# The last store of a transfer-bound kernel, cut into three parts by partitions

## Chip, core and metric

The kernel runs on one core of a Trainium2 chip. The metric is the device time of one execution in microseconds (us). The clock granted was 1.0. The experiments ran in three groups, each on a chip of its own together with the kernel before, so a time is compared with the kernel before "of its rounds".

## The reference

The inputs `y` and `dy` are fp32 tensors of shape 8 x 1024 x 8192, that is 8192 rows of 8192 numbers. The output has the same shape.

```python
softmax_x = np.exp(y)
sum_dy = np.sum(dy, axis=-1, keepdims=True)
return (dy - softmax_x * sum_dy).astype(np.float32)
```

Two tensors of 268 MB are read and one is written, and each number is used in a handful of operations: 805 MB pass through the transfer engines.

## The kernel before

The 8192 rows are 32 groups of 256 rows. A group fills a tile of 128 partitions, two rows in each, so a partition holds 64 KB that are contiguous in memory as well. Two tiles `x0` and `x1` take `dy` and become the output in place; one tile takes `y`. All transfers are issued by one queue. Only the end of the loop matters here.

```python
out_v = out.flatten_outer_dims().rearrange("(g p r) d -> g p (r d)", p=P, r=R)   # P = 128, R = 2
# ... loads, sums and pieces of exp and multiply-add cut ...
for g in range(0, G, 2):
    # ... x_ts[0] and x_ts[1] are loaded and computed ...
    for j in range(2):
        nc.sync.dma_start(out=out_v[g + j], in_=x_ts[j][:])
```

## Time and profile before

| | before |
|---|---|
| median of 4 runs | 1867.63 us (1866.89 to 1867.79) |
| transfers | 99.9% of 16 engines' span, 432 GB/s |
| VectorE, ScalarE busy | 46%, 37% |
| vector engine done with the last tile | 1837.9 us in the trace |
| first and last completion signal of the last store | 1861.20 and 1865.06 us |

The lines behind this are in the prediction below. Two further windows of the trace of the kernel before are the yardstick for later: start and end of the window in us, its length, three busy times, the clock, the share of the 16 transfer engines, GB/s.

```profile
1842.00:1846.00 4.00, 0.00 (x0) 0.00 (x0) 0.00 (x0) 1.00 0.91 393
1846.00:1850.00 4.00, 0.00 (x0) 0.00 (x0) 0.00 (x0) 1.00 1.02 442
```

No compute runs any more, and the last store flows at the full rate, 418 GB/s over the two windows. A packet is counted where it starts, so a short window may read somewhat high or low.

### The profile page before, as it was taken

How to read it: one execution, taken by the hardware profiler on the slowest of the kernel's cores; microseconds unless marked ns; L12 is line 12 of the kernel's file. 1: busy time of each engine (PE TensorE's matmuls, PEld its weight loads, DVE VectorE, ACT ScalarE, POOL GpSimd, SP SyncE). 2: the span in 40 equal slices, each digit the busy share in tenths (PEclk: the TensorE clock that was granted, in tenths of full speed). 3: DMA queues.
4: the chain of work that ended last, by engine and by line, in shares of the span. 5: the costliest groups of instructions: out<-in, count | busy, mean ns of one | idle time of the engine just before them, and what ended most of it. 6: DMA issues, size and time to landing. Idle time of an engine off the chain costs nothing.

```text
span 1865.9 us, 923 instructions
## 1 busy us (share of the span) xinstructions
DVE 859.8 (46%) x256; ACT 698.7 (37%) x321; POOL 0.2 (0%) x4
## 2 busy tenths in 40 slices
DVE  2907429074290732807328073280632806338063
ACT  2606326063260532605336052360523605236052
POOL 0000000000000000000000000000000000000000
DMA  9999999999999999999999999999999999999999
GB/s 427 424 430 427 430 447 427 427 431 445 427 427 441 426 437 434 438 431 427 437 438 429 433 428 440 434 431 437 425 438 436 433 436 425 439 433 436 434 428 391
DMA packets 16135, 805.37 MB, mean 432 GB/s; under 512 B 1792, under 2 KB 1792, under 8 KB 1792
## 3 DMA queue, kind: packets, MB, share of 16 engines
q1 hardware_dynamic: 16128, 805.31, 99.9%
q14 instruction: 7, 0.06, 0.0%
HBM read 536.87 MB, written 268.44 MB: 432 GB/s over the span
## 4 chain that ended last, share of the span: by engine, by line
DMA 64%; DVE 13%; ACT 10%; another core or an unknown queue 9%; issue 1%; SPq 0%; DVEq 0%; ACTq 0%
DMA x<-in_dy_dram 31%; DMA out_dram<-x 30%; DVE x L81 13%; ACT copied L61 6%; ACT y_t L80 4%; DMA y_t<-in_y_dram 3%; SPq L75 0%; DVEq L128 0%; ACTq L128 0%; SPq L52 0%; ACTq L80 0%; ACTq L61 0%
## 5 line engine op out<-in xcount | busy, mean ns | idle before, releaser
L81 DVE SCALAR_TENSOR_TENSOR x<-y_t,s_t,x 128x3072 f32<-128x3072 f32 (+1 forms) x192 | 579.4, 3059 | 255.7 <-ACT y_t L80 255.7
L57 DVE TENSOR_REDUCE s_t<-x 128x1 f32<-128x8192 f32 x32 | 277.8, 8682 | 722.3 <-DMA x<-in_dy_dram 722.3
L80 ACT ACTIVATE y_t<-y_t 128x3072 f32<-128x3072 f32 (+1 forms) x192 | 460.1, 2466 | 269.4 <-DMA y_t<-in_y_dram 253.2
L61 ACT ACTIVATE copied<-x 128x4096 f32<-128x4096 f32 x64 | 229.6, 3587 | 864.9 <-DMA x<-in_dy_dram 863.9
L61 ACT ACTIVATION_READ_ACCUMULATOR copied<-x 128x1 f32 x64 | 11.9, 186 | 0.0
L64 DVE TENSOR_SCALAR s_t<-half_t 128x1 f32<-128x1 f32 x32 | 6.5, 204 | 0.0
L61 ACT ACT_TABLE_LOAD x1 | 1.3, 1283 | 0.7 <-PEq L117 0.7
L117 POOL MEMSET const-bfloat16-1.0<- 128x1 bf16 x1 | 0.1, 101 | 0.0
L117 POOL MEMSET const-uint8-127<- 128x1 uint8 x1 | 0.1, 101 | 0.0
L117 POOL MEMSET const-float32-0.0<- 128x1 f32 x1 | 0.1, 98 | 0.2 <-issue 0.2
L117 POOL MEMSET const-float32-1.0<- 128x1 f32 x1 | 0.1, 98 | 0.0
## 6 DMA issues: line engine op xcount, KB each, us to landing
y_t<-in_y_dram SPq DMA_DIRECT2D x32, 4096.0 KB, 18.1
x<-in_dy_dram SPq DMA_DIRECT2D x32, 48.3
out_dram<-x SPq DMA_DIRECT2D x32, 32.5
y_t<-in_y_dram SPq DMA_DIRECT2D x16, 57.6
```

Source lines behind the costliest of these rows:

```text
L57: nc.vector.tensor_reduce(out=s_t[:, 0:1], in_=x[:, :D], axis=mybir.AxisListType.X, op=ALU.add, negate=True)
L61: nc.scalar.activation(copied[:], x[:, D + h * H : D + (h + 1) * H], COPY, accum_out=half_t[:, h : h + 1])
L64: nc.vector.tensor_scalar(out=s_t[:, 1:2], in0=half_t[:, 0:1], scalar1=half_t[:, 1:2], scalar2=-1.0, op0=ALU.add, op1=ALU.mult,)
L80: nc.scalar.activation(y_t[:, cs], y_t[:, cs], EXP)
L81: nc.vector.scalar_tensor_tensor(out=x[:, cs], in0=y_t[:, cs], scalar=s_t[:, r : r + 1], in1=x[:, cs], op0=ALU.mult, op1=ALU.add,)
L117: nc = _bacc.Bacc("TRN2", target_bir_lowering=False, num_devices=1)
```

## The change

As far as the edit shows, the intent is balance at the end. The 16 transfer engines stop 3.9 us apart; if the late engine is the one that is left out, it gets less of the last store. 15 partitions on 15 engines leave one out, 112 partitions give seven to each of the 16, and the last partition is meant to be divided evenly.

```diff
-        for j in range(2):
-            nc.sync.dma_start(out=out_v[g + j], in_=x_ts[j][:])
+        nc.sync.dma_start(out=out_v[g], in_=x_ts[0][:])
+        if g + 2 < G:
+            nc.sync.dma_start(out=out_v[g + 1], in_=x_ts[1][:])
+        else:
+            nc.sync.dma_start(out=out_v[g + 1][0:15], in_=x_ts[1][0:15, :])
+            nc.sync.dma_start(out=out_v[g + 1][15 : P - 1], in_=x_ts[1][15 : P - 1, :])
+            nc.sync.dma_start(
+                out=out_v[g + 1][P - 1 : P].rearrange("p (e w) -> p e w", e=16),
+                in_=x_ts[1][P - 1 : P, :].rearrange("p (e w) -> p e w", e=16),
+            )
```

## The prediction

The terms of its sum came to about 10 us more than before: 7.25 for the first part, about 3.5 for the second, less up to 0.75 for balance; the third part was put at 2.42 at most and left out. They were estimates. The unit is the packet of 2.418 us in the trace of before: 7.25 us are the three further packets if four take turns (4 x 2.418 = 9.67 us instead of 2.42), and about 3.5 is the middle of 2 to 5, for one or two such turns. Balance was put at -0.75 us if the late engine is the one left out (it has one packet less, but the next engine is only 0.92 us ahead of it, and gets a sixteenth of the last partition) and +0.2 if not. That packets take turns was not shown then. "Port" is, here and in all that follows, a name for whatever packets of several engines share when they slow each other.

> **What bounds the kernel now.** I read the page first: engines, slices, queues.
>
> ```profile
> span 1865.9 us, 923 instructions
> ...
> DVE 859.8 (46%) x256; ACT 698.7 (37%) x321; POOL 0.2 (0%) x4
> ...
> DMA  9999999999999999999999999999999999999999
> GB/s 427 424 430 427 430 447 427 427 431 445 427 427 441 426 437 434 438 431 427 437 438 429 433 428 440 434 431 437 425 438 436 433 436 425 439 433 436 434 428 391
> ...
> q1 hardware_dynamic: 16128, 805.31, 99.9%
> ```
>
> The reader is to see that no compute engine is busy for half of the span, and that the 16 transfer engines together are busy for 99.9% of it. 805 MB over 1865.9 us is 432 GB/s from the first slice to the last but one. So compute time, waits and issue order are hidden; only two things set the time: how many bytes one transfer engine has to move and how fast it moves them, and how unevenly the 16 engines stop. The trace's transfer records give the unit: a 64 KB row (one partition of a group: two rows of 8192 fp32) is one packet, and 2.418 us is the common duration of one, load or store, which is 65,536 B / 2.418 us = 27.1 GB/s per engine and 16 x 27.1 = 434 GB/s for all. A group of 128 partitions is 8 such packets per engine, 19.3 us.
>
> Then the end, which is all that the change touches: first the waits of the store queue from 1700 us on, then short windows from 1838 us on (the last two columns are the transfer engines' share and GB/s, counted by the packets that start in the window).
>
> ```profile
> SPq L128 <- DMA out_dram<-x: 26.6, 2, 19.2
> ```
>
> ```profile
> 1850.00:1855.00 5.00, 0.00 (x0) 0.00 (x0) 0.00 (x0) 1.00 1.03 446
> 1855.00:1860.00 5.00, 0.00 (x0) 0.00 (x0) 0.00 (x0) 1.00 0.97 419
> 1860.00:1861.00 1.00, 0.00 (x0) 0.00 (x0) 0.00 (x0) 1.00 0.76 328
> 1861.00:1862.00 1.00, 0.00 (x0) 0.00 (x0) 0.00 (x0) 1.00 0.15 66
> 1862.00:1863.00 1.00, 0.00 (x0) 0.00 (x0) 0.00 (x0) 1.00 0.15 66
> 1863.00:1864.00 1.00, 0.00 (x0) 0.00 (x0) 0.00 (x0) 1.00 0.00 0
> ```
>
> The vector engine is done with the last tile at 1837.9 us; from there the program only waits for its two last stores, 19.2 us for the second. 66 GB/s over 1 us is one 64 KB packet: from 1860 to 1861 us five packets start, then one, then a last one alone after 1862 us. The 16 completion signals of that store in the trace say the same finer: the first engine signals at 1861.20 us, the last but one at 1864.14, the last at 1865.06. The engines end 3.86 us apart. The last one is 0.92 us behind the next, and only that lone stretch is there to be won by unloading one engine. The spread was 0.65 us after the first load and grew by small irregular delays; each engine moved the same number of bytes.
>
> [...]
>
> **The change, part by part.** Bytes are the same. Issue: two stores become four; the store issues of before took 344 and 432 ns, so the two added ones cost some 0.8 us of the issuing queue, starting at 1837.9 us, while the engines are busy with the store before until 1841.9 us or later: hidden.
>
> [...]
>
> [...] Sum: 7.25 + about 3.5, less up to 0.75 of the gain, so about 10 us as the full estimate, and 6 to 7 if the second part brings no meetings.
>
> **The rivals.** (1) *The ports bind*: +6 to +12 us. [...] Against it: nothing in this trace shows a port at its limit apart from its engine, and whoever made the change expected 15 engines to run side by side. I give it 55%. (2) *The ports do not bind for reads*: only balance counts, -0.8 us if the late engine is the one unloaded, +0.2 us if not. For it: the engine's own rate explains all that is seen in before. 37%. (3) *The ports bind and the shares of the second part are interleaved* (engine e takes every sixteenth partition): [...] +25 us or more. Against it: 16 neighbours at once would be a poor way to split[...]. 8%. A new wait of the queue or of compute as the bound is out: nothing is computed after 1837.9 us, and the engines have 4 us of work queued when the parts are issued.
>
> **Range and chances.** The time before is 1867.58 us, with runs from 1866.89 to 1867.79, so noise is under 1 us. Rival 2 gives 1866.8 to 1867.8, rival 1 1873.5 to 1879.5, rival 3 about 1893 or more. The two main outcomes have a hole between them. The middle of my distribution lies at the low edge of rival 1, and I place the point there: 1873 us. The range, 1866 to 1881, holds rivals 2 and 1 whole. Two per cent is 37 us: no gain of that size exists, since the whole spread of the engines is 3.9 us, and only a bad form of rival 3 could lose it. So within 2% is all but certain.
>
> **What would show it.** In the changed kernel's trace look at the packets that start after 1838 us. If ports bind, up to 15 packets of 64 KB last toward 9.7 us instead of 2.42, the GB/s of the windows from 1842 to 1852 us falls to a third, and one engine's completions come many us before the others'. If they do not bind, every 64 KB packet stays at 2.42 us[...], and the spread of the last completions shrinks from 3.86 us to about 3. [...] The page's counts should rise by the packets of the split: 128 rows become 127 rows and 16 pieces, and the completions from 16 to 15 + 16 + 16. The prediction is wrong [...] if a packet's duration shows a sharing cost between the two cases (half-shared ports), or if the time falls by more than 1 us.

## The result

The changed kernel takes 1882.70 us (median of 4 runs, 1882.23 to 1884.27) against 1867.63 us: 15.1 us more. The ratio is 1.0083, with a 95% interval of 1.0065 to 1.0100. Ratios here are the mean time of one kernel's runs over that of the other's runs of the same rounds, so not quite the ratio of the medians. By the 2% rule it is the same; by the noise of this kernel, under 1 us in the runs before, it is clearly slower.

The page of the changed kernel first: the rate in 40 equal slices of the time, then the queue.

```profile
GB/s 423 423 425 433 434 446 424 440 425 437 436 430 439 424 444 425 444 425 439 430 437 429 433 433 432 430 436 437 429 439 427 441 430 434 432 429 439 432 437 231
...
q1 hardware_dynamic: 16144, 805.31, 99.6%
```

Only the last slice of 47 us differs: 231 GB/s where it was 391. The bytes are the same, so the whole loss lies in that slice, which reaches to the new end. The queue's packet count gives away one more thing. It rose by 16, from 16128. A store of 128 rows on 16 engines is 128 + 16 = 144 packets, data and completions; the new parts give 15 + 15, 112 + 16, and for the last partition either 16 + 16 or 1 + 1. Only the last choice makes 160. So the view as 16 pieces did not survive: the row, contiguous on both sides, went as one packet of 64 KB on one engine.

Next, what the store queue waits for from 1700 us on, and windows over the end, of the changed kernel. The first line is the waiting for the last stores: 42.8 us in total, where the kernel before had 26.6. That is 16.2 of the 16.6 us by which the two profiled runs differ.

```profile
SPq L137 <- DMA out_dram<-x: 42.8, 2, 39.5
```

```profile
1842.00:1846.00 4.00, 0.00 (x0) 0.00 (x0) 0.00 (x0) 1.00 1.15 197
1846.00:1850.00 4.00, 0.00 (x0) 0.00 (x0) 0.00 (x0) 1.00 0.43 147
1850.00:1855.00 5.00, 0.00 (x0) 0.00 (x0) 0.00 (x0) 1.00 0.82 275
1855.00:1860.00 5.00, 0.00 (x0) 0.00 (x0) 0.00 (x0) 1.00 1.10 315
1860.00:1865.00 5.00, 0.00 (x0) 0.00 (x0) 0.00 (x0) 1.00 0.75 249
1865.00:1870.00 5.00, 0.00 (x0) 0.00 (x0) 0.00 (x0) 1.00 0.83 275
1870.00:1875.00 5.00, 0.00 (x0) 0.00 (x0) 0.00 (x0) 1.00 0.53 170
1875.00:1880.00 5.00, 0.00 (x0) 0.00 (x0) 0.00 (x0) 1.00 0.13 52
```

From 1842 to 1850 us, when the first part is in flight, the rate is (197 + 147) / 2 = 172 GB/s instead of 418. Later it is 249 to 315, until 1870 us, and does not come back. The share column is higher than the rate suggests (a mean of 0.79 over these two windows, with 172 GB/s): the engines are occupied, but their packets are slow. In the transfer records 99 of 100 packets of 64 KB before the last store take at most 2.43 us; the 15 of the first part take 3.3 to 14.1 us, and many of the second part lie near 5.1 us, twice the normal.

The trace also lets one engine be recognised: after the store before, exactly one engine goes on with a packet of 2.42 us, where 15 have a slow one. It must be the one without a share in the first part; the trace has no engine numbers. It finished the store before at 1842.42 us, 1.26 us ahead of the last engine. In this execution the late engine was another one.

### The profile page after: what moved, and what is told of

Read it like the earlier page. It is cut to its first block, busy times and chain, and to the rows that moved or that the text cites. A ratio compares the mean times of both kernels' runs of the same rounds, so it can differ in the third digit from the quotient of the medians.

```text
span 1882.5 us, 925 instructions
## 1 busy us (share of the span) xinstructions
DVE 859.9 (46%) x256; ACT 698.7 (37%) x321; POOL 0.2 (0%) x4
## 4 chain that ended last, share of the span: by engine, by line
DMA 64%; DVE 13%; ACT 10%; another core or an unknown queue 9%; issue 1%; SPq 0%; DVEq 0%; ACTq 0%
DMA x<-in_dy_dram 31%; DMA out_dram<-x 30%; DVE x L81 13%; ACT copied L61 6%; ACT y_t L80 4%; DMA y_t<-in_y_dram 3%; SPq L75 0%; DVEq L137 0%; ACTq L137 0%; SPq L52 0%; ACTq L80 0%; ACTq L61 0%
```

## The experiments

**Theory A** says that the reading of the partitions is shared: some partitions lie on one port, a port delivers one 64 KB packet per 2.42 us (the time of a packet in the trace of before) whoever asks, and the parts send several engines to one port. Which partitions those are is for the probes to show. **Theory B** says that the places of the rows in memory collide. **Theory C** says that more transfers in the queue cost. **Theory D** says that the uneven shares make the time, above all the ninth packet on the engine that got the single row.

### A probe: stores alone, one at a time

The kernel's loop is replaced by one load and then single stores of 64 KB rows, each after the one before has landed. Its output is wrong, which doesn't matter for the time.

```diff
-    for g in range(0, G, 2):
-        ... (the whole loop)
+    x = x_ts[0]
+    o = out_v[G - 1]
+    load_dy(0, x)
+    for rep in range(2):
+        gate()      # a small write to the tile, which waits for the store before it
+        nc.sync.dma_start(out=o[0:128], in_=x[0:128, :])
+        gate()
+        nc.sync.dma_start(out=o[0:15], in_=x[0:15, :])
+        gate()
+        nc.sync.dma_start(out=o[36:93:4], in_=x[36:93:4, :])
+        gate()
+        nc.sync.dma_start(out=o[0:15], in_=x[36:93:4, :])
+        gate()
+        nc.sync.dma_start(out=o[36:93:4], in_=x[0:15, :])
+        ... (further sets in the same way)
```

> A probe, wrong result on purpose: one load, then stores of 64 KB rows one at a time, each waiting for the one before, twice over. Each is told by the time its packets take, between issue and completion; some 2 us of fixed time lie on top. Theory A (the SBUF ports are shared: a port gives 27.1 GB/s, one packet alone 2.42 us): 128 partitions 19.3 us of packets; 15 neighbouring partitions 9.7; 15 partitions 36,40,..,92[...], 2.4, whether their rows go to neighbouring places in HBM or to spread ones; 15 neighbouring partitions to spread rows in HBM still 9.7; 112 partitions from 15 or from 0 about 22 instead of 17; 16 neighbours 9.7; 4 neighbours (one port) 9.7, 4 partitions on four ports 2.4. Theory B (the rows' places in HBM collide, not the ports): what decides is the destination: neighbouring rows slow whatever the source, spread rows fast even from neighbouring partitions. Theory C (the queue or the number of transfers costs): all sets of 15 or 16 the same 2.4. The partition as 16 pieces in one transfer: one packet of 64 KB on one engine, 2.4 us, as the trace of the changed kernel suggests; as two transfers of 16 separate 2 KB pieces: spread over 16 engines. The last two are loads into the 15 neighbouring and the 15 spread partitions: theory A 9.7 and 2.4.

The windows from one issue to the next, in this order: 128 partitions; 15 neighbours; 15 spread (36, 40, up to 92); spread partitions to neighbouring rows in memory; neighbouring partitions to spread rows in memory; the 112 of the change; the single partition as in the change. The columns are as before, with two busy times instead of three.

```profile
22.84:43.81 20.97, 0.07 (x1) 0.00 (x0) 1.00 0.93 400
43.81:55.52 11.71, 0.07 (x1) 0.00 (x0) 1.00 0.75 84
55.52:60.24 4.72, 0.07 (x1) 0.00 (x0) 1.00 0.49 208
60.24:64.90 4.66, 0.07 (x1) 0.00 (x0) 1.00 0.50 211
64.90:76.60 11.70, 0.07 (x1) 0.00 (x0) 1.00 0.75 84
76.60:100.48 23.88, 0.07 (x1) 0.00 (x0) 1.00 0.85 307
...
168.14:171.66 3.52, 0.00 (x0) 0.00 (x0) 1.00 0.04 19
```

The four middle comparisons are the case in small. The source decides (11.7 against 4.7 us) and the destination changes nothing (11.71 and 11.70; 4.72 and 4.66). Theory B is out, and so is theory C for this transfer, since all four move 15 rows on 15 engines (15 data packets and 15 completions in the windows of both sets). The packets alone, without the fixed time around them, take 19.54, 10.31, 2.59, 2.59, 10.31 and 22.48 us in the order of the first six windows. Beside seven eighths of 19.54 = 17.10 us, the 112 partitions are 5.4 us slow. In windows that are not printed 16 neighbours took 11.72 us, four neighbours (0 to 3) 11.54, and four in steps of four (0, 4, 8, 12) 4.36. So 0 to 3 share a port, those four in steps of four do not, and 15 or 16 neighbours take as long as four at one port: I call them a four-port part, an estimate from these times. The trace shows the single partition as one data packet of 2.45 us and one completion; sent as two transfers of 16 separated 2 KB pieces it became 32 data packets. The same holds for loads: into the 15 neighbours 9.7 us of packets, into the 15 spread partitions 3.35, a little more than the 2.4 expected.

### The same end with one thing undone

**The single row truly on 16 engines.**

```diff
-            nc.sync.dma_start(
-                out=out_v[g + 1][P - 1 : P].rearrange("p (e w) -> p e w", e=16),
-                in_=x_ts[1][P - 1 : P, :].rearrange("p (e w) -> p e w", e=16),
-            )
+            for h in range(2):
+                nc.sync.dma_start(
+                    out=out_v[g + 1][P - 1 : P].rearrange("p (e h w) -> p e h w", e=16, h=2)[:, :, h],
+                    in_=x_ts[1][P - 1 : P, :].rearrange("p (e h w) -> p e h w", e=16, h=2)[:, :, h],
+                )
```

> As the change, but the last partition goes as two transfers of 16 separated 2 KB pieces each, so that it truly runs on 16 engines. Theory A (shared ports): the third part is a bystander, since its single packet ended 3 us before the last one of the second part; 1880 to 1884 us, within 1 us or so of the changed kernel's 1882.7. Theory D (the ninth packet on one engine makes the time): 2.4 us or more of the 15 come back, 1880 us or less.

It took 1884.30 us (ratio to before 1.0092, 1.0077 to 1.0107), no better than the change and 0.3 us over the range expected for a bystander (1880 to 1884). Spreading the lone packet wins nothing back.

**Equal shares on all 16 engines.**

```diff
-            ... (the three parts)
+            nc.sync.dma_start(out=out_v[g + 1][0:16], in_=x_ts[1][0:16, :])
+            nc.sync.dma_start(out=out_v[g + 1][16:128], in_=x_ts[1][16:128, :])
```

> The last store in two parts, partitions 0 to 15 and 16 to 127, each on all 16 engines with equal shares: no engine is unloaded, no single row. Theory A: still about 12 us or more over the kernel before, 1878 to 1885 us[...]. Theory D (unequal shares, k = 15 or the single row): like the kernel before, 1867 to 1868 us.

It took 1883.53 us (1.0090, 1.0073 to 1.0107). Here no engine is unloaded and none has a ninth packet, if the 16 and the 112 are shared equally, as the 112 are in the changed kernel's trace (seven packets in each chain); and the loss is all there. (k = 15 in the expectation means the 15 engines of the first part.) Theory D is out: the cost does not come from the balance. Whether the uneven shares gain a little is not shown, since the intervals of the two ratios overlap and 0.75 us is too small to tell.

**Two parts by columns.**

```diff
-            ... (the three parts)
+            for h in range(2):
+                nc.sync.dma_start(
+                    out=out_v[g + 1][:, h * D : (h + 1) * D], in_=x_ts[1][:, h * D : (h + 1) * D]
+                )
```

> The last store in two parts by columns: all 128 partitions in each, half of the row each. [...] Theory A: 1867 to 1868 us, as the kernel before. Theory C (more transfers in the queue at the end cost): slower by several us.

It took 1866.81 us, beside 1866.96 for the kernel before in the same rounds (ratio 0.9999, 0.9984 to 1.0014). One more transfer at the end cost nothing here, where each transfer holds all 128 partitions.

**Two parts by partitions.** The same number of transfers, each over half of the partitions.

```diff
-            ... (the three parts)
+            nc.sync.dma_start(out=out_v[g + 1][0:64], in_=x_ts[1][0:64, :])
+            nc.sync.dma_start(out=out_v[g + 1][64:128], in_=x_ts[1][64:128, :])
```

> The last store as partitions 0 to 63 and 64 to 127: two equal transfers on all 16 engines, as many transfers as by columns (1866.8 us)[...]. Shared ports: each half takes as long as a whole store, 15 to 19 us over the kernel before, 1882 to 1887 us. If only small or uneven parts hurt: 1867 to 1868.

It took 1885.35 us, 17.3 us over the 1868.03 of its rounds (1.0093, 1.0076 to 1.0110). This and the columns are the cleanest pair: two equal parts each. What differs is the partitions and the packets, 64 KB here and 32 KB by columns; the first probe has slow and fast sets with packets of one size, so the size is not the cause.

### A second probe: how many engines a port feeds

> A second probe, wrong result on purpose, sets of stores one after the other, twice over; times are those of the packets. If a port delivers one packet of 64 KB per 2.45 us whoever asks: partitions 0-0, 0-1, 0-2, 0-3 (one port, one to four engines) 2.5, 4.9, 7.4, 9.9 us; partitions 0 and 4, or 0 and 64, 2.5; partitions 0 and 32, 4.9 if they share a port[...], else 2.5. 32 partitions from 0: 9.9; 64 from 0 and 64 from 64: 19.5 each[...]; 64 from 32: 9.9[...]. Halves 0-63 then 64-127 queued together: 35 to 39 us, against 19.5 for 128 at once. 15 and 112 queued together: 30 to 33 us; with the last partition as well: the same within 2.5. Two full stores queued together: 39; a full store and then the three parts: 39 plus 13 to 16 if the 15 us of the changed kernel come from the transfers alone. Rival: if sharing costs only when engines start in step, the queued sets would come out well under the sums of the parts measured alone.

The edit is the same kind of loop as in the first probe, with other sets and with some stores queued together. The windows are, in order: partition 0; 0 and 1; 0 to 2; 0 to 3; 0 and 4; 0 and 32; 0 and 64; 0 to 63; 32 to 95; the halves queued together; the 15 and the 112 queued together; two full stores; a full store and the three parts.

```profile
22.93:26.67 3.74, 0.07 (x1) 0.00 (x0) 1.00 0.04 18
26.67:33.05 6.38, 0.07 (x1) 0.00 (x0) 1.00 0.10 21
33.05:42.00 8.95, 0.07 (x1) 0.00 (x0) 1.00 0.14 22
42.00:53.54 11.54, 0.07 (x1) 0.00 (x0) 1.00 0.22 23
53.54:57.90 4.36, 0.07 (x1) 0.00 (x0) 1.00 0.07 30
57.90:64.72 6.82, 0.07 (x1) 0.00 (x0) 1.00 0.09 19
64.72:68.87 4.15, 0.07 (x1) 0.00 (x0) 1.00 0.07 32
80.60:102.92 22.32, 0.07 (x1) 0.00 (x0) 1.00 0.91 188
125.21:136.87 11.66, 0.07 (x1) 0.00 (x0) 1.00 0.84 360
136.87:179.16 42.29, 0.07 (x1) 0.00 (x0) 1.00 0.95 198
179.16:216.39 37.23, 0.07 (x1) 0.00 (x0) 1.00 0.79 224
253.44:293.84 40.40, 0.07 (x1) 0.00 (x0) 1.00 0.96 415
293.84:349.84 56.00, 0.07 (x1) 0.00 (x0) 1.00 0.88 300
```

Each further engine at one port adds some 2.6 us, so the rate stands at 18 to 23 GB/s while the number of engines quadruples. By packets alone the last of one to four engines is done after 2.45, 5.13, 7.69 and 10.26 us. Partition 32 collides with 0 (6.82 us, where 0 alone took 3.74), partitions 4 and 64 do not (4.36 and 4.15). 64 partitions from 0 need as long as 128 do (20.58 us of packets, 204 GB/s, against 19.54 for the 128 of the first probe); 64 partitions from 32 need half of that (9.87 us, 425 GB/s). By an estimate, at the 27.1 GB/s of a packet alone these are the rates of 7.5 and 15.7 packets at a time: I count the first set as lying on eight ports and the second on sixteen. By packets alone, the 15 and 112 queued together take 35.8 us, more than their 10.31 + 22.48 = 32.8 alone, and with the single row 35.6. That is over the range expected for it (30 to 33): queued behind each other, these two do 3.0 us worse than their sum. The halves were over their range too (40.5 us of packets, where 35 to 39 were expected), but alone they take 20.58 us each, so their 40.5 is a little under the sum. The last line reproduces the case outside the kernel: 56.00 - 40.40 = 15.6 us, where the kernel lost 15.1.

### Where in the queue the small part stands

**112 partitions before 16.**

```diff
-            ... (the three parts)
+            nc.sync.dma_start(out=out_v[g + 1][0:112], in_=x_ts[1][0:112, :])
+            nc.sync.dma_start(out=out_v[g + 1][112:128], in_=x_ts[1][112:128, :])
```

> The last store as partitions 0 to 111 and then 112 to 127, both on all 16 engines. Shared ports: still slow[...]; 1877 to 1884 us. If the loss came from the small part standing first and delaying what follows: close to 1868.

It took 1875.14 us, 7.1 us over the 1868.03 of its rounds (1.0039, 1.0024 to 1.0054). This missed what I expected of theory A, 1877 to 1884, from below, and it is not the 1868 of the rival either. Sharing alone, as a sum of costs, does not explain it; the order counts.

**The change's own three parts, the 15 after the 112.**

```diff
-            nc.sync.dma_start(out=out_v[g + 1][0:15], in_=x_ts[1][0:15, :])
             nc.sync.dma_start(out=out_v[g + 1][15 : P - 1], in_=x_ts[1][15 : P - 1, :])
+            nc.sync.dma_start(out=out_v[g + 1][0:15], in_=x_ts[1][0:15, :])
```

> The three parts of the change in another order: 112 partitions first, then the 15, then the single one. If the costs of the parts simply add: 1880 to 1884 us as in the change. If the four-port part costs most when all engines meet it in step, and less when they come to it spread over some 10 us, as the run with 112 before 16 suggests (1875.1 us): 1873 to 1878 us.

It took 1874.00 us, 6.8 us over the 1867.17 of its rounds (1.0038, 1.0021 to 1.0055). Its windows show what the order does.

```profile
1842.00:1846.00 4.00, 0.00 (x0) 0.00 (x0) 0.00 (x0) 1.00 0.87 328
1846.00:1850.00 4.00, 0.00 (x0) 0.00 (x0) 0.00 (x0) 1.00 1.06 410
1850.00:1855.00 5.00, 0.00 (x0) 0.00 (x0) 0.00 (x0) 1.00 0.99 380
1855.00:1860.00 5.00, 0.00 (x0) 0.00 (x0) 0.00 (x0) 1.00 0.91 367
1860.00:1865.00 5.00, 0.00 (x0) 0.00 (x0) 0.00 (x0) 1.00 0.96 197
1865.00:1870.00 5.00, 0.00 (x0) 0.00 (x0) 0.00 (x0) 1.00 0.03 13
```

With the 112 first, the rate from 1842 to 1860 us is 328 to 410 GB/s, where the change had 147 to 315. In the change, 15 engines come to four ports within 2.2 us of each other (1841.5 to 1843.7 us), and are all held there for 3.3 to 14.1 us. In the transfer records never more than 16 data packets are under way at once, and at the end of each of the 15 another one starts, within 0.12 us (0.003 us after the one of 14.1 us). So, as I read it, an engine takes one packet at a time, and the 15 cannot go on to other ports although their next packets lie ready. At the end, they come to the four ports over 6.4 us (1857.7 to 1864.1 us in the trace of this run), and meanwhile the others still work elsewhere. Of the 15.1 us, about 8 hang on this order. That ports stand idle meanwhile is my reading of the rates (172 GB/s from 1842 to 1850 us, against 418 before); that held engines are the reason is argued, and no run shows it by itself.

### One port per engine, in place

**Partitions 32 to 95 first.**

```diff
-            ... (the three parts)
+            nc.sync.dma_start(out=out_v[g + 1][32:96], in_=x_ts[1][32:96, :])
+            nc.sync.dma_start(out=out_v[g + 1][0:32], in_=x_ts[1][0:32, :])
+            nc.sync.dma_start(out=out_v[g + 1][96:128], in_=x_ts[1][96:128, :])
```

> The last store as partitions 32 to 95 (four per engine[...]), then 0 to 31, then 96 to 127 (two per engine[...]). Shared ports[...]: the first part costs nothing, each of the others 9.7 us instead of 4.8, partly overlapping; 7 to 11 us over, 1874 to 1879 us, so clearly less than the halves although it has one part more. [...]

It took 1875.09 us, 7.1 us over the 1868.03 of its rounds (1.0038, 1.0023 to 1.0053), far better than the two halves although there is a part more. In its trace the packets of 32 to 95 take 2.42 us, and only those of the two outer parts stretch, to 5.1 us and more.

```profile
1842.00:1846.00 4.00, 0.00 (x0) 0.00 (x0) 0.00 (x0) 1.00 1.02 442
1846.00:1850.00 4.00, 0.00 (x0) 0.00 (x0) 0.00 (x0) 1.00 1.02 442
1850.00:1855.00 5.00, 0.00 (x0) 0.00 (x0) 0.00 (x0) 1.00 1.23 354
1855.00:1860.00 5.00, 0.00 (x0) 0.00 (x0) 0.00 (x0) 1.00 0.83 236
```

442 GB/s for as long as the middle part lasts, then 236, about half of that, for the outer parts.

**Fifteen spread partitions in place of fifteen neighbours.**

```diff
-            nc.sync.dma_start(out=out_v[g + 1][32:96], in_=x_ts[1][32:96, :])
+            nc.sync.dma_start(out=out_v[g + 1][36:93:4], in_=x_ts[1][36:93:4, :])
+            nc.sync.dma_start(out=out_v[g + 1][32:33], in_=x_ts[1][32:33, :])
+            nc.sync.dma_start(out=out_v[g + 1][33:94:4], in_=x_ts[1][33:94:4, :])
+            nc.sync.dma_start(out=out_v[g + 1][34:95:4], in_=x_ts[1][34:95:4, :])
+            nc.sync.dma_start(out=out_v[g + 1][35:96:4], in_=x_ts[1][35:96:4, :])
```

> The middle 64 partitions of the run with three parts (32 to 95, then 0 to 31, then 96 to 127: 1875.1 us) go as 15 partitions 36,40,..,92 on 15 engines, partition 32 alone on one engine, and three transfers of every fourth partition; the other two parts are kept. Shared ports: [...]15 partitions on 15 engines cost nothing by themselves; 1874 to 1878 us, the upper end if the single row makes one engine late by its 2.4 us. Rival: if 15 rows on 15 engines, or transfers of one row per engine, are slow in place whatever their ports: 1880 us or more.

It took 1878.93 us, 11.8 us over the 1867.17 of its rounds (1.0063, 1.0048 to 1.0078). The expectation was missed by 1 us upwards, though not as far as the rival's 1880. The part that the run was made for came out: the first packet of every engine after the store before takes 2.42 to 3.5 us here, against up to 14.1 in the change. It is 4.7 us slower than the run before it by the differences to each one's own rounds. One packet of 2.4 us on a single engine is the obvious share of it; the rest stays open.

## Why the prediction was wrong

It was wrong in size: 1873 us with a range up to 1881, and 1882.7 measured. Its main mechanism, that neighbouring partitions share ports, was right (10.31 us for the 15 neighbours, 2.59 for the 15 spread). The step that failed is the sum of the main case, "7.25 + about 3.5, less up to 0.75": it gave about 10 us, at most 12, where 15.1 were measured. Step by step:

- **What bounds the kernel** held. All else is hidden, and issue cost nothing: the run by columns equals the kernel before.
- **The first part** was put at 7.25 us. Alone it measured 10.31 - 2.59 = 7.7 us. Nearly right; sharing has a small cost of its own (four packets at one port take 10.26 us, not 4 x 2.45 = 9.8).
- **The second part** is a mis-sized term. "About 3.5" is the middle of the range of 2 to 5, and the end is set by the unluckiest engine; two turns at a port would be 2 x 2.42 = 4.8 us. Alone the part measured 5.4 us.
- **The adding** failed most. It treats the parts as if each began afresh. Queued together they took 35.8 us, 3.0 more than apart. Instead of 10 us: 7.7 + 5.4 + 3.0 = 16.1 us in the probe, 15.6 behind another store, 15.1 in the kernel. That an engine held for up to 14.1 us starts its later packets that much later was not in the sum at all. The order runs show that about 8 us hang on what stands first; that the holding is the reason is argued.
- **The balance gain**, 0.75 us, could not be seen. Equal shares cost 16.6 us and the change 15.1, with intervals that overlap, and the engine that was unloaded was not the late one in the changed kernel's trace.
- **The third part** was taken to run on 16 engines. The packet count shows one packet on one engine. Spreading it over 16 engines won nothing.
- **The rivals**: that ports do not bind for reads got 37%, and the first probe refutes it outright. Interleaved shares, at +25 us, did not occur. **The point** of 1873 was placed just under the main case (1873.5 to 1879.5) to hedge against the first of these; even the upper end of the main case, +12, was short by 3 us.
- The signs named for the main case came in the main: first packets of 3.3 to 14.1 us, five of the 15 over the 9.7 that four packets at one port explain, a rate of a third to a half from 1842 to 1850 us, and one engine ahead (its last completion signal at 1862.5 us, the last of all at 1881.7). Those over 9.7 are not explained by the sum; packets of the second part that come to the same ports are an obvious cause, not separated here.

None of the versions beats the kernel before; the columns only equal it. Every version here with parts by partitions lost 6.8 us or more, and the whole spread of the engines is 3.9 us, so I see no gain to be had by moving rows off a late engine; this is argued, not run.

## What to carry to other kernels

Splitting the store of a whole tile by partitions can cost half the rate (188 GB/s for 64 partitions from 0, 360 from 32, in windows of the second probe): split such a transfer by columns, which cost nothing here (1866.81 us beside 1866.96), or by sets of partitions that a probe shows to run at full rate, as 32 to 95 did and 0 to 15 or 0 to 63 did not. Before balancing engines, find out which one is late and whether the shape still runs on the engines it is meant for; the packet count tells. Where a slow part cannot be avoided, try it last in the queue: here that saved 8 us, in my reading because a held engine (up to 14.1 us on one packet) holds what is queued behind it.
